# Norm scale applied by a diagonal matrix in the transposes, stores of the normed rows issued by ACT, token rows of the folds loaded beside the second projection

## The chip, the cores and the metric

The kernel runs on one core of a Trainium2 chip. A core has five engines that each work through their own instructions in order: TensorE (PE: matrix products, PEld its weight loads), VectorE (DVE), ScalarE (ACT), GpSimd (POOL) and SyncE (SP, which here only issues transfers). ACT and POOL issue transfers too. The metric is the device time of one execution in microseconds.

## The reference

Two layers of a trunk work on 1280 tokens (1024 of a sample, 256 of a prompt) of width 1024. Layer 0 mixes by differential attention and an RWKV-7 recurrence, layer 1 by a Fourier transform over positions and channels; each layer ends with a gated FFN of inner width 2816. What the change touches are the norms and the residual sums around these:

```python
def rmsnorm(x, g):
    y = xf * lax.rsqrt(jnp.mean(xf * xf, axis=-1, keepdims=True) + RMS_EPS)
    return y * g

def trunk_layer(l, x, mod, rope, ctx, P):
    h = rmsnorm(x, gains[0]) * (1 + scale_m) + shift_m
    if l % 2 == 0:
        m, new_ctx = even_mixer(h, l, rope, ctx, P)
    else:
        m, new_ctx = fourier_mix(h, P["w_out_odd"][l // 2]), None
    x = x + gate_m * rmsnorm(m, gains[1])
    h = rmsnorm(x, gains[2]) * (1 + scale_f) + shift_f
    f = conv_ffn(h, P["w_ffn_in"][l], P["ffn_conv"][l], P["ffn_conv_b"][l], P["w_ffn_out"][l])
    x = x + gate_f * rmsnorm(f, gains[3])
```

## The kernel before

The tokens are worked on in ten blocks of 128 rows, of 1024 elements each. Matrix products are made of three products of a high and a low part (`mm3`, L145 to L147), and the parts are made by `split` (a cast on ACT, L140, and a difference on DVE, L141). A scheduler sets the order of the instructions on every engine from the program's text and the pools' buffers.

Four places matter.

The *output stage of layer 0* (some 1640 to 1760 us) makes the mixer's output `of` for each block, adds it to the token rows, and norms the sum for the FFN: DVE writes the scaled rows to a tile of their own, `nxs` (L292); `norm_store` transposes them in eight blocks of 128x128 into PSUM (L303, `n_ps`); ACT (L307) and DVE (L311) in turn write `nt` from that with the modulation; and POOL stores `nt` to `h_d` in memory (L315). The FFN loads it from there as `tc` (L1260).

The *second projection of each FFN* (in layer 0 some 2380 to 2618 us) goes through three groups of blocks: two of four blocks and one of two. Each group runs over the 22 slices of the inner width; for each slice it loads a piece of the weight (`e_raw`) and of the activations (`e_m`), splits them into `e_hi` and `e_lo`, and adds to accumulators in the PSUM banks a, b, c and d. At a group's end `finish` copies them out (`fo`), norms and gates them, adds the token rows `rx`, and stores the sum.

The *folds* (from 2618 us) open layer 1. Each of five folds loads two blocks of token rows (`nx`), makes the reciprocal norm, builds `dg`, a diagonal matrix of the norms, on POOL (L1630), multiplies the rows by it (`xt_ps`, L1638), copies that out (`fh`) and multiplies it with the transform's table (`ab_ps`, L1650).

The *output stage of layer 1* (some 2720 to 2860 us) runs `outputs` for five pairs of blocks: the prompt's pair first, then the sample's pairs `lt` 0, 3, 1 and 2, in an order of steps written out by hand. Each pair makes a difference `fmn` and a sum `fpl`, gates both, adds `fmn` to the first block's rows (on POOL, L1894) and the flipped `fpl` to the second block's (L1900), and stores both to `x2` (L1895 and L1903; the trace calls the memory `x_d`). L1903 stores from row `s0` on, and `s0` is 1 for the last pair of a sequence:

```python
            s0 = 1 if lt == ntl - 1 else 0
            nc.sync.dma_start(out=x2[t0s[1] + s0:t0s[1] + 128], in_=x[s0:128])
```

That is so for the prompt's pair and for `lt` 3. Here the norm's scale is written over the token rows themselves (L1879), and `norm_store` transposes them from there.

Of the kernel before, what the change touches and what calls it, by code (L numbers as in the profile page):

```python
# [18 lines left out]
D = 1024  # L19
# [12 lines left out]
RING = 5  # L32
# [67 lines left out]
def hybrid_step(ctx: ExitStack, tc: tile.TileContext, i: dict, o: dict):  # L100
# [183 lines left out]

    def norm_scale(pl, tj, f, xs):

        jk = pl.tile([128, D], F32, tag=tj[0], bufs=tj[1], name="njk")
        ss = pl.tile([128, 1], F32, tag="nss", bufs=4, name="nss")
        nc.scalar.activation(jk, f, AF.Square, accum_out=ss)
        rs = pl.tile([128, 1], F32, tag="nrs", bufs=4, name="nrs")  # L290
        rsqrt(rs, ss, 1.0 / D, RMS_EPS, pl, 1)
        nc.vector.tensor_scalar(out=xs, in0=f, scalar1=rs, op0=ALU.mult, scalar2=None)  # L292

    def norm_store(pl, tt, ps_tile, xs, t0, hd, A, B):

# [3 lines left out]
        for k0 in range(0, KD, 4):  # L299
            ps = ps_tile()  # L300
            t = pl.tile([128, 4, 128], F32, tag=tt[0], bufs=tt[1], name="nt")
            for e in range(4):
                nc.tensor.transpose(ps[:, e, :], xs[:, (k0 + e) * 128:(k0 + e + 1) * 128], ident)  # L303
            for e in range(4):
# [5 lines left out]
                else:  # L310
# [3 lines left out]
                    )  # L314
            nc.gpsimd.dma_start(out=hd[half, :, k0:k0 + 4, c:c + n], in_=t[:, :, :n])  # L315

# [337 lines left out]

    def out_product(fw, fo, po, t0, nf=2):

# [623 lines left out]
    with ExitStack() as st:  # L1280
# [6 lines left out]
        for n, j in enumerate((0, 4, 1, 8, 9, 5, 2, 6, 3, 7)):  # L1287
            t0 = j * 128
            f = fs.pop(0) if fs else out_product(fw, fo, po, t0)
            if todo:  # L1290
                norm_store(xp, ("nt", 3), n_ps, *todo.pop(), hd, A, B)
            if n == 6:
                strassen_tokens(opa, xp, hd, 0, 256)
            finish_tile(xp, f, gg, None, lambda a, n: x_d[0][a:a + n], t0)
            xs = xp.tile([128, D], F32, tag="nxs", bufs=2, name="nxs")
            norm_scale(xp, ("njk", 1), f, xs)
            todo.append((xs, t0))

# [8 lines left out]
    def ffn(l, src, dst_rows, st, fw, hd, opa, late, groups, then):  # L1307
# [3 lines left out]
        with st:  # L1311
# [120 lines left out]
            def out_operands(f, js, early):  # L1432

                hl = lambda: [
                    (fw if early else dp).tile(
                        [128, 512], F32R, tag=("f_" if early else "e_") + q, bufs=RING if early else 15, name="e_" + q
                    ) for q in ("hi", "lo")
# [35 lines left out]
            def finish(j, pss):  # L1473
                t0 = j * 128
                f = dp.tile([128, D], F32, tag="fo", bufs=3, name="fo")
                for hf in range(2):
                    nc.scalar.copy(f[:, hf * 512:hf * 512 + 512], pss[hf])
                x = dp.tile([128, D], F32, tag="rx", bufs=4, name="rx")
                nc.sync.dma_start(out=x, in_=x_rows(src, t0, 128))
# [11 lines left out]
            for gi, js in enumerate(groups):  # L1491
                acc = {j: [bank("abcd"[2 * (e % 2) + hf]) for hf in range(2)] for e, j in enumerate(js)}
                tail = gi == len(groups) - 1
                kept = {}
                for f in range(NFF):
                    if gi == 0 and f == 2:
                        st_u.close()
                        st_h.close()
                        beside = then()
                        dp = pool(st, "fd")  # L1500
                        for cnd in range(2):
                            g = dp.tile([128, D], F32, name=f"gg{cnd}")
                            nc.gpsimd.dma_start(out=g, in_=mod_d[l][1, cnd].partition_broadcast(128))
                            gg.append(g)
                    if gi == 0 and f == 6:
                        beside()
                    ops = out_operands(f, js, gi == 0 and f < 2)
                    if tail and f >= NFF - 4:
                        kept[f] = ops
# [58 lines left out]
    def fourier_tables():  # L1568

        ab = pool(st_t, "qa")  # L1570
        bs = pool(st_b, "qb")
        F["A"] = mod_cols(1, 1)
        F["B"] = mod_cols(1, 0)
# [21 lines left out]
    with ExitStack() as st:  # L1595
# [18 lines left out]
        s1 = pool(st_b, "qx")  # L1614
        flip = flip_tile(s1)

        def fold(cnd, n):
# [3 lines left out]
            for m, a in enumerate((base + 1 + 128 * n, base + L - 128 * (n + 1))):  # L1621
                x = s1.tile([128, D], F32, tag="nx", bufs=4, name="nx")
                nc.sync.dma_start(out=x, in_=x1[a:a + 128])
                jk = s1.tile([128, D], BF16, tag="njk", bufs=1, name="njk")
                ss = s1.tile([128, 1], F32, tag="nss", bufs=4, name="nss")
                nc.scalar.activation(jk, x, AF.Square, accum_out=ss)
                rs = s1.tile([128, 1], F32, tag="nrs", bufs=4, name="nrs")
                rsqrt(rs, ss, 1.0 / D, RMS_EPS, s1, 1)
                d = s1.tile([128, 128], F32, tag="dg", bufs=4, name="dg")
                nc.gpsimd.tensor_scalar(out=d, in0=(ident, flip)[m], scalar1=rs, scalar2=None, op0=ALU.mult)  # L1630
# [229 lines left out]
        def outputs(cnd, lt, g, xp, flip):  # L1860
# [3 lines left out]
            t0s = base + l0, base + L - 128 * (lt + 1)  # L1864
            xs = []
            fm = xp.tile([128, D], F32, tag="fmn", bufs=1, name="fmn")
# [10 lines left out]
            def scale(m):  # L1877
                x = xs[m]
                nc.vector.tensor_scalar(out=x, in0=x, scalar1=rms(xp, x), scalar2=None, op0=ALU.mult)  # L1879

            def norm(m):
                norm_store(xp, ("nt", 3), E["n"], xs[m], t0s[m], hd, A, B)

# [9 lines left out]
            gated(xp, fm, g)  # L1893
            nc.gpsimd.tensor_tensor(out=xs[0], in0=xs[0], in1=fm, op=ALU.add)  # L1894
            nc.sync.dma_start(out=x2[t0s[0]:t0s[0] + 128], in_=xs[0])  # L1895
# [114 lines left out]
```

## Time and profile before

| what | value |
| --- | --- |
| runs, us | 3745.22, 3733.98, 3738.79 (median 3738.79) |
| the profiled execution, us | 3751.75 |
| its span, from the first to the last instruction, us | 3749.9 |
| mean granted clock of TensorE | 0.935 of full speed |
| PE busy | 91% of the span |
| DVE busy | 62% |
| ACT busy | 43% |
| POOL busy | 16% |

The profiled execution is one of its own; its time stands beside the span to show what lies around it. Shares of busy time are averages over the whole span. The granted clock is 1.00 at 2.4 GHz and half of that at 1.2 GHz.

### The profile page before, as it was taken

What the parts mean: (1) busy time and instruction counts of PE and PEld (TensorE: products, weight loads), DVE (VectorE), ACT (ScalarE), POOL (GpSimd) and SP (SyncE); (2) the same over time, 40 slices, a digit from 0 to 9 for tenths busy, and PEclk for the clock granted to TensorE, in tenths of its full rate; (3) what the DMA queues carried; (4) which work ended last, traced back from release to release, by engine and by line L of the source; (5) the groups of instructions that cost most, each with busy time, mean ns of one, the idle gap of its engine ahead of it and who ended that gap; (6) DMA issues with size and microseconds to landing.
All of it is one profiled execution on the core that took longest, in us unless ns stands there. A gap on an engine that the chain in (4) does not pass through costs nothing. (4 is left out here: it accounts for less than half of the span.)

```text
span 3749.9 us, 58125 instructions
## 1 busy us (share of the span) xinstructions
PE 3430.5 (91%) x21672; PEld 2914.6 (78%) x21672; DVE 2320.2 (62%) x5039; ACT 1611.7 (43%) x3248; POOL 581.6 (16%) x883
## 2 busy tenths in 40 slices
PE   6999999889898967788999999999875999999999
PEld 5888887655554656667899999887754899999887
DVE  4277677745464657547877776545547877776345
ACT  4266566753444443435433322335434433333334
POOL 3111112421221212022000002201122000001000
PEclk9999999879797967889999999999887999999999
DMA  6322313233243200155222224855335212225455
GB/s 214 99 86 88 94 61 101 69 93 110 90 121 94 79 19 17 55 155 171 90 70 74 65 74 149 263 189 181 131 104 154 89 63 72 73 66 180 143 187 184
DMA packets 313435, 413.83 MB, mean 110 GB/s; under 512 B 62770, under 2 KB 228626, under 8 KB 313152
## 3 DMA queue, kind: packets, MB, share of 16 engines
q1 hardware_dynamic: 234784, 308.58, 26.7%
q0 software_dynamic: 29968, 81.88, 6.3%
q10 hardware_dynamic: 48400, 19.65, 2.1%
q8 instruction: 171, 2.80, 0.3%
q14 instruction: 112, 0.92, 0.1%
HBM read 321.21 MB, written 90.83 MB: 110 GB/s over the span
## 5 line engine op out<-in xcount | busy, mean ns | idle before, releaser
L140 ACT CAST f_hi<-ws 128x512 fp32r<-128x512 f32 x192 | 119.1, 621 | 360.8 <-PE ua_ps L146 156.5
L1392 POOL DMA_DIRECT2D m_d<-md x176 | 95.5, 543 | 1001.3 <-DVE md L1391 1001.1
L141 DVE TENSOR_TENSOR e_lo<-e_m,e_hi 128x512 fp32r<-128x512 f32 (+1 forms) x132 | 79.3, 600 | 247.6 <-ACT e_hi L140 247.6
L140 ACT CAST f_hi<-f_raw 128x512 fp32r<-128x512 f32 x144 | 89.2, 621 | 300.7 <-PE ud_ps L146 106.1
L192 PE MATMUL ada_ps<-ada_w,csil 128*32 128x512 f32 x384 | 174.2, 728 | 27.4 <-DMA ada_w<-in_w_ada 25.9
L145 PE MATMUL f_ps<-hh,w_hi 128*128 128x512 f32 (+1 forms) x552 | 198.5, 360 | 0.5 <-ACT nk L451 0.5
L140 ACT CAST e_hi<-e_m 128x512 fp32r<-128x512 f32 (+1 forms) x132 | 72.6, 550 | 292.0 <-PE uc_ps L147 265.2
L147 PE MATMUL f_ps<-hh,w_lo 128*128 128x512 f32 (+1 forms) x552 | 197.3, 357 | 0.0
L146 PE MATMUL f_ps<-hl,w_hi 128*128 128x512 f32 (+1 forms) x552 | 197.3, 357 | 0.0
L141 DVE TENSOR_TENSOR e_lo<-e_raw,e_hi 128x512 fp32r<-128x512 f32 x264 | 174.0, 697 | 23.3 <-ACT e_hi L140 23.1
L140 ACT CAST e_hi<-e_raw 128x512 fp32r<-128x512 f32 x264 | 151.1, 618 | 61.3 <-DMA e_raw<-in_w_ffn_out 32.5
L141 DVE TENSOR_TENSOR f_lo<-ws,f_hi 128x512 fp32r<-128x512 f32 x192 | 133.7, 697 | 44.6 <-ACT f_hi L140 44.5
L141 DVE TENSOR_TENSOR f_lo<-f_raw,f_hi 128x512 fp32r<-128x512 f32 x144 | 98.9, 688 | 99.8 <-ACT f_hi L140 99.6
L531 DVE TENSOR_REDUCE nm<-sc_ps 128x1 f32<-128x512 f32 (+1 forms) x208 | 118.8, 583 | 54.2 <-PE sc_ps L527 53.1
L532 ACT ACTIVATE e<-sc_ps,nm 128x512 f32<-128x512 f32 (+1 forms) x208 | 126.1, 608 | 56.8 <-DVE nm L531 53.9
L1380 DVE SCALAR_TENSOR_TENSOR cv<-gp,cw,cv 128x1282 f32<-128x1282 f32 x88 | 134.4, 1548 | 0.0
L145 PE MATMUL ua_ps<-b11h,f_hi 128*128 128x256 f32 (+1 forms) x352 | 111.7, 317 | 10.9 <-ACT nt L307 6.4
L145 PE MATMUL ub_ps<-b21h,f_hi 128*128 128x256 f32 (+1 forms) x352 | 111.5, 317 | 8.2 <-ACT b21h L140 7.7
L527 PE MATMUL sc_ps<-ks,qs 128*128 128x512 f32 (+1 forms) x384 | 110.9, 382 | 6.7 <-ACT e L532 6.7
L145 PEld LDWEIGHTS f_ps<-hh,w_hi 128*128 128x128 f32 x552 | 104.2, 189 | 16.2 <-DVE qr L441 1.0
L146 PE MATMUL ua_ps<-b11l,f_hi 128*128 128x256 f32 (+1 forms) x352 | 111.2, 316 | 5.6 <-DVE b11l L141 5.6
L146 PEld LDWEIGHTS f_ps<-hl,w_hi 128*128 128x128 f32 x552 | 104.2, 189 | 14.7 <-issue 0.5
(656 smaller groups left out, 11253.6 us busy)
## 6 DMA issues: line engine op xcount, KB each, us to landing
e_raw<-in_w_ffn_out SPq DMA_DIRECT2D x132, 512.0 KB, 4.2
f_raw<-in_w_ffn_in SPq DMA_DIRECT2D x96, 512.0 KB, 4.0
ada_w<-in_w_ada SPq DMA_DIRECT2D x160, 256.0 KB, 2.9
m_d<-md POOLq DMA_DIRECT2D x88, 192.0 KB, 2.4
w_raw<-in_w_in_even SPq DMA_DIRECT2D x23, 512.0 KB, 5.2
m_d<-md POOLq DMA_DIRECT2D x88, 128.0 KB, 2.0
e_m<-m_d SPq DMA_DIRECT2D x44, 256.0 KB, 4.3
lo_in<-fb_d SPq DMA_DIRECT2D x40, 256.0 KB, 3.0
```

The source lines that it names most:

```text
L140: nc.scalar.copy(hi, src)
L141: nc.vector.tensor_tensor(out=lo, in0=src, in1=hi, op=ALU.subtract)
L145: nc.tensor.matmul(ps, lhsT=a[0], rhs=b[0], start=first, stop=False)
L146: nc.tensor.matmul(ps, lhsT=a[0], rhs=b[1], start=False, stop=False)
L147: nc.tensor.matmul(ps, lhsT=a[1], rhs=b[0], start=False, stop=last)
L192: nc.tensor.matmul(ps[32 * q:32 * q + 32], lhsT=csil[:, k0 + k, :], rhs=w[:, k, :], start=(k0 < 4), stop=(k0 >= 4),)
L527: nc.tensor.matmul(ps[:, :nn], lhsT=qs[:, m, a, :], rhs=ks[m][:, n0:n0 + nn], start=(a == 0), stop=(a == 1),)
L531: nc.vector.reduce_max(nm[:, m, j:j + 1], ps[:, :nn], axis=AX.X, negate=True)
L532: nc.scalar.activation(e[:, :nn], ps[:, :nn], AF.Exp, bias=nm[:, m, j:j + 1], accum_out=sm[:, m, j:j + 1])
L1380: nc.vector.scalar_tensor_tensor(out=cv, in0=gp[:, j:T + 2 + j], scalar=cw[:, j, f + e:f + e + 1], in1=cv, op0=ALU.mult, op1=ALU.add,)
L1392: nc.gpsimd.dma_start(out=m_d[f + e, :, half, c * 256:c * 256 + n], in_=md)
```

## The change

The scale of the norm is no longer written to the rows. `scale_matrix` (layer 0) and `scale` (layer 1) write a 128x128 matrix `dg` with the norms on its diagonal, on DVE, and `norm_store` multiplies the unscaled rows by it, with `matmul` in place of `transpose`. Its stores are issued by ACT instead of POOL. In `outputs` the sum of rows and `fmn` moves from POOL to DVE. In the second projection the ring of operands has 12 buffers instead of 15 (a set is three), `rx` 2 instead of 4, the last group holds back three slices instead of four, a group of two blocks uses the banks c and d alone, and the gates are loaded at slice 4. The folds' token rows and norms get a pool of their own, `qn`, that is opened with the transform's tables, ahead of the second projection's end.

```diff
-    def norm_scale(pl, tj, f, xs):
+    def scale_matrix(pl, tj, f):
...
-        nc.vector.tensor_scalar(out=xs, in0=f, scalar1=rs, op0=ALU.mult, scalar2=None)
+        dg = pl.tile([128, 128], F32, tag="dg", bufs=2, name="dg")
+        nc.vector.tensor_scalar(out=dg, in0=ident, scalar1=rs, scalar2=None, op0=ALU.mult)
+        return dg
...
-                nc.tensor.transpose(ps[:, e, :], xs[:, (k0 + e) * 128:(k0 + e + 1) * 128], ident)
+                nc.tensor.matmul(
+                    ps[:, e, :], lhsT=x[:, (k0 + e) * 128:(k0 + e + 1) * 128], rhs=dg, start=True, stop=True
+                )
...
-            nc.gpsimd.dma_start(out=hd[half, :, k0:k0 + 4, c:c + n], in_=t[:, :, :n])
+            nc.scalar.dma_start(out=hd[half, :, k0:k0 + 4, c:c + n], in_=t[:, :, :n])
...
-    def out_product(fw, fo, po, t0, nf=2):
+    def out_product(fw, fo, po, t0, nf=3):
...
-                        [128, 512], F32R, tag=("f_" if early else "e_") + q, bufs=RING if early else 15, name="e_" + q
+                        [128, 512], F32R, tag=("f_" if early else "e_") + q, bufs=RING if early else 12, name="e_" + q
...
-                x = dp.tile([128, D], F32, tag="rx", bufs=4, name="rx")
+                x = dp.tile([128, D], F32, tag="rx", bufs=2, name="rx")
...
-                acc = {j: [bank("abcd"[2 * (e % 2) + hf]) for hf in range(2)] for e, j in enumerate(js)}
+                acc = {j: [bank(("cd" if len(js) == 2 else "abcd")[(2 * e + hf) % min(4, len(js))]) for hf in range(2)] for e, j in enumerate(js)}
...
+                    if gi == 0 and f == 4:
...
-                    if tail and f >= NFF - 4:
+                    if tail and f >= NFF - 3:
...
+        F["sn"] = pool(st_b, "qn")
...
-                x = s1.tile([128, D], F32, tag="nx", bufs=4, name="nx")
+                x = sn.tile([128, D], F32, tag="nx", bufs=4, name="nx")
...
-                d = s1.tile([128, 128], F32, tag="dg", bufs=4, name="dg")
+                d = sn.tile([128, 128], F32, tag="dg", bufs=4, name="dg")
...
-                x = xs[m]
-                nc.vector.tensor_scalar(out=x, in0=x, scalar1=rms(xp, x), scalar2=None, op0=ALU.mult)
+                d = xp.tile([128, 128], F32, tag="dg", bufs=1, name="dg")
+                nc.vector.tensor_scalar(out=d, in0=ident, scalar1=rms(xp, xs[m]), scalar2=None, op0=ALU.mult)
+                dgs.append(d)
...
-            nc.gpsimd.tensor_tensor(out=xs[0], in0=xs[0], in1=fm, op=ALU.add)
+            nc.vector.tensor_tensor(out=xs[0], in0=xs[0], in1=fm, op=ALU.add)
```

The order of SP's issues in the output stage of layer 1, around the second store of 127 rows, was this (`x_d_60` is `x1`, `x_d_61` is `x2`; `nx` are loads of token rows, `tc` what the FFN reads):

```order
L1890 DMA nx<-x_d_60 128x1024
L1895 DMA x_d_61<-nx 128x1024
L1903 DMA x_d_61<-nx 127x1024
L1260 DMA tc<-h_d_70 128x256
L1890 DMA nx<-x_d_60 128x1024 x2
```

With the change it is this:

```order
L1897 DMA nx<-x_d_60 128x1024
L1264 DMA tc<-h_d_70 128x256
L1902 DMA x_d_61<-nx 128x1024
L1910 DMA x_d_61<-nx 127x1024
L1897 DMA nx<-x_d_60 128x1024 x2
```

The load of `tc` has moved ahead of the store of 127 rows; two loads of token rows stand behind the store in both.

ACT's order from the end of layer 0's second projection to the first fold was this (`rjk` and `njk` are the sums of squares of the projection's and of the folds' norms):

```order
L1477 COPY fo<-uc_ps 128x512
L1488 DMA x_d_60<-fo 128x1024
L1477 COPY fo<-ud_ps 128x512
L1482 ACTIVATE rjk,rss<-fo 128x1024
L1488 DMA x_d_60<-fo 128x1024
L1626 ACTIVATE njk,nss<-nx 128x1024 x4
L1678 ACTIVATE zj,zs<-zx 2x1024
L1723 CAST w64s<-w64r 72x1024
L1645 COPY fh<-xt_ps 128x512 x2
```

With the change it is this:

```order
L1479 COPY fo<-uc_ps 128x512
L1479 COPY fo<-ud_ps 128x512
L1484 ACTIVATE rjk,rss<-fo 128x1024
L1490 DMA x_d_60<-fo 128x1024 x2
L1651 COPY fh<-xt_ps 128x512
L1684 ACTIVATE zj,zs<-zx 2x1024
```

The four norms of the folds and the cast of `w64s` no longer stand between the last store and the copy `fh`.

## Rows read from the trace of the kernel before

**Rows 1.** The page's busy times: engine, us, share of the span, instructions.

```profile
PE 3430.5 (91%) x21672; PEld 2914.6 (78%) x21672; DVE 2320.2 (62%) x5039; ACT 1611.7 (43%) x3248; POOL 581.6 (16%) x883
```

**Rows 2.** Busy time in stretches: length, PE, PEld, DVE, ACT, POOL, clock, DMA share, GB/s.

```profile
1700.00:1720.00 20.00, 20.00 (x96) 16.61 (x95) 14.88 (x35) 11.47 (x29) 4.43 (x7) 1.00 0.69 230
...
2580.00:2600.00 20.00, 20.00 (x90) 16.55 (x89) 13.60 (x26) 11.93 (x25) 0.00 (x0) 1.00 0.93 290
...
2800.00:2820.00 20.00, 6.73 (x23) 5.04 (x24) 5.66 (x11) 5.59 (x13) 5.29 (x6) 0.59 0.25 83
```

**Rows 3.** Waits from 2725 to 2860 us: who for what, total us, times, longest.

```profile
PE n_ps L303 <- ACT nt L307: 41.0, 4, 17.1
PE n_ps L303 <- DVE nx L1879: 10.9, 1, 10.9
...
DVE nx L1879 <- DMA x_d<-nx: 35.5, 4, 19.0
...
ACT b11h L140 <- DMA tc<-h_d: 23.5, 2, 20.7
```

**Rows 4.** Timeline of SP's issues: start us, length us, line, what, count.

```profile
2737.93 0.24 SPq L1903 DMA_DIRECT2D x_d<-nx  x1
...
2787.69 0.24 SPq L1903 DMA_DIRECT2D x_d<-nx  x1
2789.75 7.69 SPq L1260 DMA_DIRECT2D tc<-h_d  x1
2797.54 18.05 SPq L1890 DMA_DIRECT2D nx<-x_d  x2
```

**Rows 5.** Timeline of DVE; in brackets the idle time before and its releaser.

```profile
2761.68 0.75 DVE L1879 TENSOR_SCALAR nx<-nx,nrs 128x1024 f32<-128x1024 f32 x1 [15.31 <-DMA x_d<-nx]
...
2811.08 0.75 DVE L1879 TENSOR_SCALAR nx<-nx,nrs 128x1024 f32<-128x1024 f32 x1 [19.01 <-DMA x_d<-nx]
...
2815.89 1.29 DVE L1853 SCALAR_TENSOR_TENSOR fmn<-fmn,nrs,gg 128x1024 f32<-128x1024 f32 x1 [0.75 <-POOL nrs L137]
```

**Rows 6.** Transfers from 2735 to 2765 us, GB/s in 40 equal slices.

```profile
GB/s 0 344 355 0 5 22 22 33 16 22 22 27 27 27 27 27 22 88 231 287 131 45 28 26 23 26 27 27 27 27 22 27 27 27 27 5 0 0 0 0
```

**Rows 7.** Timeline of PE, at the folds' start and at a run of transposes.

```profile
2631.02 2.07 PE L1638 MATMUL xt_ps<-dg,nx 128*128 128x128 f32 x8 [12.48 <-POOL dg L1630]
...
2639.60 0.79 PE L1650 MATMUL ab_ps<-fcs,fh 128*128 128x128 f32 x2 [2.25 <-ACT fh L1645]
...
2743.53 1.03 PE L303 MATMUL n_ps<-ident,nx 128*128 128x128 f32 x8
```

**Rows 8.** Timeline of ACT and its queue, at the folds' start and later.

```profile
2627.22 0.33 ACTq L1488 DMA_DIRECT2D x_d<-fo  x1
...
2638.97 0.57 ACT L1645 COPY fh<-xt_ps 128x512 f32<-128x512 f32 x1
...
2826.50 5.69 ACTq L1322 DMA_DIRECT2D cw<-in_ffn_conv  x1
```

**Rows 9.** Instructions by line: ns least/median/most, first and last start, form.

```profile
L303 PE MATMUL n_ps<-ident,nxs x72: 270/272/476, 1655.1 to 1741.9; 128*128 128x128 f32 x72
...
L1201 DVE TENSOR_TENSOR of<-of,px x10: 1215/1218/1224, 1646.5 to 1749.7; 128x1024 f32<-128x1024 f32 x10
...
L1638 PE MATMUL xt_ps<-dg,nx x160: 274/275/579, 2631.0 to 2674.7; 128*128 128x128 f32 x160
...
L1879 DVE TENSOR_SCALAR nx<-nx,nrs x10: 732/753/755, 2737.9 to 2881.0; 128x1024 f32<-128x1024 f32 x10
...
L1894 POOL TENSOR_TENSOR nx<-nx,fmn x5: 2360/2392/2657, 2732.6 to 2841.8; 128x1024 f32<-128x1024 f32 x5
```

**Rows 10.** Transposes from 1668 to 1745 us, by line.

```profile
L303 PE MATMUL n_ps<-ident,nxs x56: 270/272/329, 1676.0 to 1741.9; 128*128 128x128 f32 x56
```

**Rows 11.** Stores of `h_d` (L315), from issue to landing.

```profile
DMA to landing us min/median/max: 2.7/3.7/7.1
```

**Rows 12.** Timeline of POOL, the transform's second table.

```profile
2623.24 2.87 POOL L1535 TENSOR_TENSOR fcn<-fcn,mod 128x1024 f32<-128x1024 f32 x1
```

More of the change, by code (lines that the diff above doesn't have):

```diff
@@ L291, in norm_scale, with norm_store @@
         rsqrt(rs, ss, 1.0 / D, RMS_EPS, pl, 1)
-        nc.vector.tensor_scalar(out=xs, in0=f, scalar1=rs, op0=ALU.mult, scalar2=None)
-    def norm_store(pl, tt, ps_tile, xs, t0, hd, A, B):
+        dg = pl.tile([128, 128], F32, tag="dg", bufs=2, name="dg")
+        nc.vector.tensor_scalar(out=dg, in0=ident, scalar1=rs, scalar2=None, op0=ALU.mult)
+        return dg
+    def norm_store(pl, tt, ps_tile, x, dg, t0, hd, A, B):
         cnd, p = (0, t0) if t0 < LS else (1, t0 - LS)
@@ L1294, in hybrid_step @@
             finish_tile(xp, f, gg, None, lambda a, n: x_d[0][a:a + n], t0)
-            xs = xp.tile([128, D], F32, tag="nxs", bufs=2, name="nxs")
-            norm_scale(xp, ("njk", 1), f, xs)
-            todo.append((xs, t0))
+            todo.append((f, scale_matrix(xp, ("njk", 1), f), t0))
     def norm_last(bank):
@@ L1571, in fourier_tables @@
         bs = pool(st_b, "qb")
+        F["sn"] = pool(st_b, "qn")
+        F["sn"].tile([128, 1], F32, tag="nss", bufs=4, name="nss")
         F["A"] = mod_cols(1, 1)
@@ L1614, in hybrid_step @@
         s1 = pool(st_b, "qx")
-        flip = flip_tile(s1)
+        sn = F["sn"]
+        flip = flip_tile(sn)
         def fold(cnd, n):
@@ L1621, in fold @@
             for m, a in enumerate((base + 1 + 128 * n, base + L - 128 * (n + 1))):
-                x = s1.tile([128, D], F32, tag="nx", bufs=4, name="nx")
+                x = sn.tile([128, D], F32, tag="nx", bufs=4, name="nx")
                 nc.sync.dma_start(out=x, in_=x1[a:a + 128])
-                jk = s1.tile([128, D], BF16, tag="njk", bufs=1, name="njk")
-                ss = s1.tile([128, 1], F32, tag="nss", bufs=4, name="nss")
+                jk = sn.tile([128, D], BF16, tag="njk", bufs=1, name="njk")
+                ss = sn.tile([128, 1], F32, tag="nss", bufs=4, name="nss")
                 nc.scalar.activation(jk, x, AF.Square, accum_out=ss)
-                rs = s1.tile([128, 1], F32, tag="nrs", bufs=4, name="nrs")
-                rsqrt(rs, ss, 1.0 / D, RMS_EPS, s1, 1)
-                d = s1.tile([128, 128], F32, tag="dg", bufs=4, name="dg")
+                rs = sn.tile([128, 1], F32, tag="nrs", bufs=4, name="nrs")
+                rsqrt(rs, ss, 1.0 / D, RMS_EPS, sn, 1)
+                d = sn.tile([128, 128], F32, tag="dg", bufs=4, name="dg")
                 nc.gpsimd.tensor_scalar(out=d, in0=(ident, flip)[m], scalar1=rs, scalar2=None, op0=ALU.mult)
@@ L1864, in outputs @@
             t0s = base + l0, base + L - 128 * (lt + 1)
-            xs = []
+            xs, dgs = [], []
             fm = xp.tile([128, D], F32, tag="fmn", bufs=1, name="fmn")
@@ L1877, in scale @@
             def scale(m):
-                x = xs[m]
-                nc.vector.tensor_scalar(out=x, in0=x, scalar1=rms(xp, x), scalar2=None, op0=ALU.mult)
+                d = xp.tile([128, 128], F32, tag="dg", bufs=1, name="dg")
+                nc.vector.tensor_scalar(out=d, in0=ident, scalar1=rms(xp, xs[m]), scalar2=None, op0=ALU.mult)
+                dgs.append(d)
             def norm(m):
-                norm_store(xp, ("nt", 3), E["n"], xs[m], t0s[m], hd, A, B)
+                norm_store(xp, ("nt", 3), E["n"], xs[m], dgs[m], t0s[m], hd, A, B)
             half(0)
```

## The prediction

> **What bounds the kernel now.** I read the busy times first, then the busy time by stretches of 20 us, then the waits inside the stretches that fall short, then the single waits in order of time. TensorE is busy for 3430.5 of 3749.9 us [rows 1], so what counts is where it stops. In the second projection of the first layer's FFN it is busy for 20.00 of 20 us at full clock, with the DMA engines at 0.93; in the first layer's output stage it is also at 20.00 of 20 [rows 2]. Nothing in those two places may get later. The loose place is the second layer's output stage (2720 to 2860 us): the stretch from 2800 has 6.73 us of TensorE at a granted clock of 0.59 [rows 2].
>
> The waits of that stage say why [rows 3]. TensorE stands 41.0 us, 4 times, at `n_ps` for ACT's `nt`, and 10.9 us for DVE's `nx`; DVE stands 35.5 us for the store `x_d<-nx`; ACT stands once for 20.7 us for `tc<-h_d`. They are one story, told in the order of time by the timeline. DVE scales the token rows in place, so it must wait until the store of the same rows has read them. Most of these stores are short, but two move 127 rows instead of 128. The first is issued at 2737.93 and DVE goes on at 2761.68 after 15.31 us; the second is issued at 2787.69 and DVE goes on at 2811.08 after 19.01 us [rows 4, 5]. From issue to release that is 23.75 and 23.39 us. While the first runs the DMA engines move only 22 to 33 GB/s for most of the time [rows 6]. What SP issues behind the second one sticks too: the load of `tc` at 2789.75 has an issue of 7.69 us, and two loads of token rows fill 18.05 us from 2797.54 [rows 4].
>
> A second loose place is the start of the folds: TensorE's first `xt_ps` matmul waits 12.48 us for `dg` from 2618.54 to 2631.02, and its first `ab_ps` matmul starts at 2639.60, after ACT's copy `fh` at 2638.97 [rows 7, 8].
>
> **The change, part by part.**
>
> *Second layer's output stage.* The scale becomes `dg = ident * rs`, which writes no token row, so neither 15.31 nor 19.01 us has a reason left on DVE. TensorE bounds the gain. It had other work during the first wait and stood 10.9 us of it [rows 3]; of its four waits for `nt` the longest, 17.1 us [rows 3], lies beside the second (by its length: the other three share 23.9). Upper end: 10.9 + 17.1 = 28 us. What is late next is the second store itself. It has the same 127 rows, the loads of the next pair of row blocks (`lt` 1) stand right behind it on SP, and the order puts `tc` ahead of it now. If everything up to it comes 10.9 us earlier, it is issued at 2776.8 and, with 23.4 us, ends at 2800.2. DVE's sum `nx + fmn` then waits for rows that stuck behind it. That end is 10.9 us earlier than 2811.08; and the two gates that ran after the wait, the last ending at 2815.89 + 1.29 = 2817.18 [rows 5], can run ahead of it. Of these 6.1 us I count 5.6, since the rows land a little after the store. Lower end: 5 us, if the wait for rows holds DVE as long as the old wait did. I take 10.9 + 5.6 = **16.5 us less**.
>
> *POOL's sum moves to DVE.* 2392 ns on POOL become about 1218 ns on DVE, by the same sum elsewhere [rows 9], 5 times; and ten scales of 753 ns become ten `dg`. A 128x128 scale on DVE from SBUF is not in the rows; it lies between nothing and the 753 ns of the scale with eight times the columns [rows 9]; I take 0.3 us, since a part of the cost will not shrink with the columns. Where DVE stands in the chain that is up to 5 x 1.17 + 10 x 0.45 = 10 us; most lies beside TensorE's work or under the waits that I have counted. I take **2 us less** (0 to 4 beyond the waits).
>
> *Transposes become matmuls.* The same kind of matmul stands in the folds: 160 records of 275 ns for 80 instructions, so each runs twice over the array, against one record of 272 ns for one transpose [rows 9]. Eight transposes in a run take 1.03 us at full clock [rows 7], so they are (1.03 - 0.27) / 7 = 0.109 us apart. One more pass is 0.109 us; 160 of them are 17.4 us of TensorE if all were on its path. In the output stage of layer 0 seven tiles of 8 (56 records) lie between 1676 and 1742 us [rows 10], where TensorE is at 20.00 of 20 [rows 2]: 7 x 0.87 = **6.1 us more**. The other 13 tiles stand where TensorE waits for eviction anyway, which hides them; without that cover they are 11.3 us more.
>
> The Trainium skill (Perfetto Trace Analysis, Transposes) says that a logical transpose should be a transpose instruction and not a standard matmul. The two passes in the row agree that the matmul costs more; charged everywhere, the rule would make the sum 11.3 us worse.
>
> *Stores of `h_d` on ACT.* 40 issues leave POOL. They land in 2.7 to 7.1 us [rows 11]. On ACT a store stands right behind the `nt` that it stores, which saves POOL's turn, but ACT's queue holds the table loads `cw`, one of which occupies the issuing queue for 5.69 us [rows 8]; stores behind it wait, and what loads `tc` for the FFN waits for them. The issue that leaves POOL saves nothing by itself, since POOL is not on the path; I count 0, with 3 us either way in each layer, less than one landing.
>
> The Trainium skill (DMA: Bandwidth & Descriptors, Issuing engines are not separate DMA queues) says that another issuing engine saves only the sequencer's time, since all end on the same 16 DMA engines. No run here shows it yet for these stores; by it the term is 0 as well.
>
> *Second projection.* Rings go from five operand sets to four, `rx` from 4 to 2 buffers, the two-token group uses two banks' pairs only, the folds' four loads come beside it. 90 matmuls in 20 us [rows 2] are 0.222 us each; one step of the two-token group has 12, 2.7 us, so four sets are 10.8 us ahead, five 13.5. The step needs 640 KB; DMA is at 0.93 and 290 GB/s in the last group [rows 2], and 2 MB of token rows at that rate are 7.2 us of DMA time. At each group's change the first tokens need banks that are copied late. I take **2 us more** for both layers together: nothing below (TensorE cannot be faster than 20.00 of 20), 7.2 above.
>
> *Folds.* Rows, norms and four `dg` are done before the last matmul, so the first `xt_ps` can follow at 2618.5. Then ACT's `fh` copy holds it: in the new order it stands behind both stores of `fo`, and the second of these came at 2627.22 [rows 8]. So `fh` starts at 2627.22 + 0.33 = 2627.55 instead of 2638.97: **11.4 us less**. POOL's table product ends at 2623.24 + 2.87 = 2626.11 [rows 12], before that. Bounds: 0, if the loads come too late, to 13 (12.48 and a little clock). The later folds keep their pace.
>
> Sum: -16.5 - 2 + 6.1 + 0 + 2 - 11.4 = **-21.8 us** on the profiled execution's 3751.75 us (the span and 1.85 us around it), to 3730. That execution was 12.96 us above the median of the runs; -0.58% of 3738.79 is **3717 us**. About 0.3% (11 us) is what a measurement of this kernel can tell from no change.
>
> **Rivals.**
>
> *The wait comes back under another name.* The 127-row store lasts as before; rows for the next pair and ACT's cast of `tc` wait behind it, and the output stage gains only 5. Sum -10.3, 3728 us. For it: SP's queue is in order, and the loads filled 18.05 us behind the store [rows 4]. Against: DVE's other work goes first. The Trainium skill (DMA: Bandwidth & Descriptors, Why a DMA increments its semaphore by 16 and not by 1) says that 127 partitions put a transfer on one DMA engine; the 22 to 33 GB/s agree, and by it the store stays as long as it is.
>
> *Everything opens.* Output stage -28, folds -13, sums -4, the extra passes hidden by later evictions: -45, 3694 us. Against: the full stretch at 1700 has no slack.
>
> *Slower: the second projection runs out of operands.* One mechanism: four sets and the nearly full DMA engines hold the steps of the two-token groups back. There are 22 steps in each layer, 44 in all. The gains elsewhere are 21.8 + 2 = 23.8; it decides from 23.8 / 44 = 0.54 us on each 2.7 us step. At 0.8 us it is 35.2 - 23.8 = +11.4, 3750 us. For it: DMA at 0.93 [rows 2]. Against: 640 KB at 290 GB/s are 2.2 us of the 2.7, and the extra rows are one burst of 7.2 us.
>
> *The folds' part doesn't do what it says* (their loads still wait): -10.4, again 3728.
>
> **How the numbers follow.** My forecast (within 10 us of -21.8) gets 0.45, the returned wait 0.20, everything open 0.17, the folds not moved 0.08, slower 0.10. Faster by over 0.3%: 0.42 of the first, 0.17, and a third of the two at -10: 0.69. Slower by over 0.3%: the last, 0.10. The rest, 0.21, is within 0.3%. The range goes from 3692 (just under everything open) to 3742 (the operands short by 0.6 us a step).
>
> **What would show it.** In the new profile DVE's 35.5 us for `x_d<-nx` must be gone; if my step is right, DVE or ACT wait instead for `nx<-x_d` behind the second 127-row store, and TensorE's waits at `n_ps` fall from 52 to some 30 us. The first `xt_ps` starts within 3 us of the last matmul and the first `ab_ps` near 11 us earlier than before, relative to that matmul. Records of the transposes double. TensorE stays at 20.00 of 20 in the second projection. The prediction is wrong if TensorE shows waits there, if `nt` waits for stores on ACT's queue, or if the layer-0 output stage grows by more than 10 us.

## The result and the profile after

| | median, us | lowest to highest | runs |
| --- | --- | --- | --- |
| before, on the same chip | 3737.38 | 3728.24 to 3745.22 | 7 |
| changed | 3715.44 | 3706.24 to 3727.19 | 7 |

The ratio is 0.9946, with a 95% interval of 0.9927 to 0.9966: 20 us less (13 to 27). The changed kernel's profiled execution took 3722.7 us, 29.05 us less than that of before; some 7 us of those are that the earlier one lay further above its median (14.4 us against 7.3).

First the page's span and busy times (answer to [rows 1]), then the stretches that answer to [rows 2], with those of layer 1's output stage from 2720 us on. Columns as there.

```profile
span 3720.9 us, 58403 instructions
...
PE 3441.2 (92%) x21832; PEld 2932.1 (79%) x21832; DVE 2317.2 (62%) x5044; ACT 1609.4 (43%) x3248; POOL 532.2 (14%) x838
```

```profile
1700.00:1720.00 20.00, 18.51 (x88) 14.63 (x87) 15.88 (x42) 13.63 (x34) 3.49 (x4) 1.00 0.73 226
...
2560.00:2580.00 20.00, 17.99 (x80) 14.58 (x79) 15.72 (x24) 9.73 (x20) 2.74 (x3) 1.00 0.95 323
2580.00:2600.00 20.00, 20.00 (x90) 16.56 (x89) 13.12 (x25) 12.85 (x26) 1.16 (x2) 1.00 0.90 297
...
2720.00:2740.00 20.00, 20.00 (x93) 15.16 (x91) 13.04 (x23) 9.35 (x19) 3.15 (x6) 1.00 0.35 129
2740.00:2760.00 20.00, 20.00 (x105) 16.10 (x105) 12.70 (x29) 10.57 (x22) 3.30 (x6) 1.00 0.41 120
2760.00:2780.00 20.00, 20.00 (x100) 16.18 (x99) 10.16 (x20) 8.14 (x16) 2.20 (x4) 1.00 0.43 132
2780.00:2800.00 20.00, 6.91 (x35) 4.99 (x33) 7.53 (x16) 4.95 (x10) 1.31 (x8) 0.75 0.33 115
```

TensorE has 160 records more and 11 us more of busy time, in a shorter span. The first wait in the output stage has gone (2720 to 2780 is full); one long hole is left, from 2780. The second projection has got a small dent at 2560. What the waits say in that output stage, in the order TensorE (from 2690 us on), DVE and ACT (2700 to 2860 us; answer to [rows 3]):

```profile
PE n_ps L305 <- ACT nt L311: 23.6, 3, 13.6
...
DVE nx L1901 <- DMA nx<-x_d: 11.2, 1, 11.2
DVE nt L315 <- DMA h_d<-nt: 10.4, 3, 3.6
...
ACT b11h L140 <- DMA tc<-h_d: 2.8, 2, 1.7
```

DVE's 35.5 us for `x_d<-nx` are gone, and TensorE's 51.9 us at `n_ps` are 23.6. In their place DVE stands 11.2 us for token rows, `nx<-x_d`. SP's timeline and DVE's show where (answer to [rows 4, 5]), and the transfers from 2765 to 2805 us, in slices of 1 us, what went on meanwhile (answer to [rows 6]):

```profile
2762.96 0.33 SPq L1264 DMA_DIRECT2D tc<-h_d  x1
...
2767.36 0.24 SPq L1910 DMA_DIRECT2D x_d<-nx  x1
2767.72 10.54 SPq L1897 DMA_DIRECT2D nx<-x_d  x2
```

```profile
2793.75 1.22 DVE L1901 TENSOR_TENSOR nx<-nx,fmn 128x1024 f32<-128x1024 f32 x1 [11.17 <-DMA nx<-x_d]
```

```profile
GB/s 373 16 0 12 16 52 221 220 85 23 28 23 146 314 227 343 80 155 130 242 65 26 27 28 23 28 23 28 24 25 91 406 29 225 299 303 277 263 316 368
```

The second store of 127 rows starts at 2767.36, the rows for the next pair stand behind it, and DVE has them at 2793.75, 26 us later. For nine slices the engines move 23 to 28 GB/s, as before. `tc` went ahead of the store; ACT waits 2.8 us for it in place of 23.5.

The folds' start (PE and ACT; answer to [rows 7, 8]), and the prices of the new instructions (answer to [rows 9, 11]):

```profile
2620.20 1.95 PE L1644 MATMUL xt_ps<-dg,nx 128*128 128x128 f32 x16
2629.80 0.80 PE L1656 MATMUL ab_ps<-fcs,fh 128*128 128x128 f32 x2 [7.65 <-ACT fh L1651]
```

```profile
2628.79 0.33 ACTq L1490 DMA_DIRECT2D x_d<-fo  x1
2629.16 0.59 ACT L1651 COPY fh<-xt_ps 128x512 f32<-128x512 f32 x1 [6.99 <-DVE z L1697]
```

```profile
L305 PE MATMUL n_ps<-dg,of x144: 270/275/377, 1655.7 to 1741.4; 128*128 128x128 f32 x144
...
L1885 DVE TENSOR_SCALAR dg<-ident,nrs x10: 276/278/287, 2728.0 to 2862.7; 128x128 f32<-128x128 f32 x10
...
L319 ACTq DMA_DIRECT2D h_d<-nt x40: 366/367/5151, 1663.4 to 2869.0; - x40
...
DMA to landing us min/median/max: 2.3/3.2/15.2
```

144 records stand where there were 72. A `dg` takes 0.278 us. A store of `h_d` costs ACT 0.367 us to issue, but one took 5.151, at 2801.78 between the table loads `cw`. One landed after 15.2 us: it is one of the two issued from 2736.67 on, behind the first store of 127 rows (2729.00) and long before the tables.

**The time by stages.** Whole executions spread by some 20 us; stages between two fixed matmuls tell more. The marks are the first start of the first `o_ps` product, of the first FFN product `ua_ps<-b11h`, of the first product of the second projection `ua_ps<-e_hi`, of the first `pq_ps<-fclsh,ab0ch` (which reads the folds' results), and the last start of `ua_ps<-b11h`, which ends the second layer's first projection. For the kernel before, and then for the changed one (columns as in [rows 9]):

```profile
L145 PE MATMUL o_ps<-o_hi,oyhi x160: 388/389/796, 1601.3 to 1738.6; 128*128 128x512 f32 x160
...
L145 PE MATMUL ua_ps<-b11h,f_hi x352: 277/336/689, 1748.6 to 3419.6; 128*128 128x256 f32 x88, 128*128 128x384 f32 x88
L145 PE MATMUL ua_ps<-e_hi x220: 389/389/397, 2319.1 to 3733.7; 128*128 128x512 f32 x110
...
L145 PE MATMUL pq_ps<-fclsh,ab0ch x8: 278/283/387, 2682.1 to 2718.9; 128*128 128x258 f32 x4, 128*128 128x256 f32 x4
```

```profile
L145 PE MATMUL o_ps<-o_hi,oyhi x160: 387/389/796, 1603.0 to 1739.0; 128*128 128x512 f32 x160
...
L145 PE MATMUL ua_ps<-b11h,f_hi x352: 277/336/690, 1748.1 to 3390.3; 128*128 128x256 f32 x88, 128*128 128x384 f32 x88
L145 PE MATMUL ua_ps<-e_hi x176: 389/389/397, 2318.7 to 3648.6; 128*128 128x512 f32 x176
...
L145 PE MATMUL pq_ps<-fclsh,ab0ch x8: 278/283/386, 2672.0 to 2710.4; 128*128 128x258 f32 x4, 128*128 128x256 f32 x4
```

The same marks in every run below, one profiled execution each, in us; the last column is the ratio of the times to the kernel before on the same chip, with its interval:

| kernel | layer 0 output stage | first projection | second projection and folds | layer 1 output stage to the end of its first projection | rest | ratio |
| --- | --- | --- | --- | --- | --- | --- |
| before | 147.3 | 570.5 | 363.0 | 737.5 | 330.3 | 1 |
| changed | 145.1 | 570.6 | 353.3 | 718.3 | 330.6 | 0.9946 (0.9927 to 0.9966) |
| changed again (`c0_after`) | 143.8 | 570.3 | 354.1 | 718.1 | 330.7 | 0.9950 (0.9934 to 0.9965) |
| `e1_inplace` | 144.0 | 570.0 | 353.7 | 734.5 | 330.9 | 0.9989 (0.9972 to 1.0006) |
| `e2_split_before` | 142.9 | 568.1 | 362.0 | 702.8 | 330.2 | 0.9913 (0.9889 to 0.9936) |
| `e3_split_after` | 144.4 | 571.2 | 354.6 | 703.4 | 330.5 | 0.9895 (0.9875 to 0.9915) |
| `e5_folds_late` | 145.1 | 570.4 | 359.2 | 718.4 | 331.0 | 0.9960 (0.9946 to 0.9974) |
| `e4_pool_stores` | 141.7 | 571.7 | 353.4 | 717.0 | 330.6 | 0.9918 (0.9893 to 0.9944) |
| `e6_layer0_scaled` | 137.8 | 569.2 | 354.3 | 718.0 | 330.7 | 0.9911 (0.9891 to 0.9931) |
| `e11_cw_rows` | 142.9 | 570.3 | 352.8 | 711.6 | 330.9 | 0.9914 (0.9893 to 0.9936) |
| `e10_split_cw_rows` | 140.5 | 570.0 | 354.3 | 695.8 | 330.7 | 0.9863 (0.9842 to 0.9885) |
| `e13_nf2` | 149.6 | 570.9 | 356.9 | 719.0 | 330.6 | 0.9955 (0.9938 to 0.9972) |
| `e14_all` | 136.9 | 568.0 | 352.5 | 696.7 | 330.4 | 0.9852 (0.9827 to 0.9877) |
| `e15_all_pool` | 134.2 | 570.5 | 352.1 | 700.6 | 329.9 | 0.9875 (0.9852 to 0.9897) |

How far a stage of the same code spreads can be read off the table: the layer 0 output stage is 143.8 to 145.1 in the five kernels that have the changed kernel's code there, and 147.3 and 142.9 in the two that have the code of before; second projection and folds are 352.8 to 354.6 in eight that have the changed kernel's code there, 356.9 in a ninth (`e13_nf2`), and 363.0 and 362.0 with the code of before; the layer 1 stage is 718.0 to 719.0 in five. The profile of before lies 14.4 us above its median and that of the changed kernel 7.3, so these two rows differ in sum by some 7 us more than the medians do. Ratios stand against runs of the kernel before on the same chip; for `e4_pool_stores`, `e6_layer0_scaled`, `e11_cw_rows` and `e10_split_cw_rows` that median was 3746.82 us, against 3737.38 to 3739.95 us for the others, so between these groups the stages are the better measure.

### The profile page after: what moved, and what is told of

Same layout as the page of the kernel before. It is cut to its first block, busy times and chain, and to the rows that moved or that the text cites. A ratio compares the mean times of both kernels' runs of the same rounds, so it can differ in the third digit from the quotient of the medians.

```text
span 3720.9 us, 58403 instructions
## 1 busy us (share of the span) xinstructions
PE 3441.2 (92%) x21832; PEld 2932.1 (79%) x21832; DVE 2317.2 (62%) x5044; ACT 1609.4 (43%) x3248; POOL 532.2 (14%) x838
## 5 line engine op out<-in xcount | busy, mean ns | idle before, releaser
L145 PE MATMUL ua_ps<-b11h,f_hi 128*128 128x256 f32 (+1 forms) x352 | 111.8, 318 | 14.4 <-ACT b11h L140 8.0
L145 PE MATMUL ub_ps<-b21h,f_hi 128*128 128x256 f32 (+1 forms) x352 | 111.2, 316 | 10.9 <-ACT b21h L140 10.3
L145 PEld LDWEIGHTS f_ps<-hh,w_hi 128*128 128x128 f32 x552 | 104.2, 189 | 16.2 <-DVE qr L445 1.0
## 6 DMA issues: line engine op xcount, KB each, us to landing
m_d<-md POOLq DMA_DIRECT2D x88, 128.0 KB, 2.0
```

The lines of the kernel that those rows point to most:

```text
L145: nc.tensor.matmul(ps, lhsT=a[0], rhs=b[0], start=first, stop=False)
```

## The experiments

**Back to the scale in place, in layer 1 alone (`e1_inplace`).**

```diff
-                d = xp.tile([128, 128], F32, tag="dg", bufs=1, name="dg")
-                nc.vector.tensor_scalar(out=d, in0=ident, scalar1=rms(xp, xs[m]), scalar2=None, op0=ALU.mult)
-                dgs.append(d)
+                x = xs[m]
+                nc.vector.tensor_scalar(out=x, in0=x, scalar1=rms(xp, x), scalar2=None, op0=ALU.mult)
+                dgs.append(None)
```

(`None` makes `norm_store` use the transpose instruction, so the second passes of layer 1 go as well.)

> The changed kernel, but layer 1's scale is written over the token rows again and its blocks are transposed by the transpose instruction. Theory (DVE waits for the store of 127 rows only because it overwrites what the store reads): DVE stands 30 us or more for x_d<-nx again, the output stage of layer 1 loses some 18 us against the changed kernel, and what is left against the kernel before is the folds' part, about 10 us (ratio near 0.997). Rival (the gain of that stage comes from the new order, from DVE's sum or from the stores on ACT): the wait stays short, and the ratio stays near the changed kernel's 0.9946.

DVE's waits in the output stage of this kernel:

```profile
DVE nx L1888 <- DMA x_d<-nx: 34.0, 3, 19.9
```

The wait is back with 34.0 us, the stage is 734.5 us, 16.2 more than in the changed kernel, and the ratio is 0.9989. DVE's sum, the new order and the stores on ACT are all still in this kernel; together they are worth 3 us of the stage. The rival falls. The ratio leaves 4 us of gain, with an interval of -2 to 10, where some 10 were expected; the stage with the folds is 9.3 us shorter than in the profile of before.

**Only the store's shape, in the kernel before (`e2_split_before`).**

```diff
-            nc.sync.dma_start(out=x2[t0s[1] + s0:t0s[1] + 128], in_=x[s0:128])
+            for r0, r1 in ((1, 113), (113, 128)) if s0 else ((0, 128),):
+                nc.sync.dma_start(out=x2[t0s[1] + r0:t0s[1] + r1], in_=x[r0:r1])
```

> The kernel before, in which each store of 127 rows is issued as one of 112 rows and one of 15. Theory (the store's 23.4 us are those of its shape, and the in-place scale is harmless beside a quick store): each part lands in some 2.5 to 5 us, DVE's 35.5 us for x_d<-nx fall under 8, and the kernel gains 18 to 28 us by itself (ratio 0.9925 to 0.995), as much as the changed kernel does as a whole, without any of its parts. Rival (a slow stretch of all transfers there, whatever the shape): the stores stay above 15 us and the ratio is 1.000.

DVE's wait in that stage, and the transfers from 2714 to 2734 us in slices of 0.5 us (the first store of this shape is issued at 2717.10):

```profile
DVE nx L1879 <- DMA x_d<-nx: 1.1, 2, 0.7
```

```profile
GB/s 0 0 377 401 270 0 0 90 279 287 344 90 0 0 0 0 0 16 0 0 0 0 0 0 0 0 73 293 164 293 219 0 0 0 0 0 0 0 0 0
```

The 508 KB go through in some 2.5 us at up to 344 GB/s, where one transfer of 127 rows needed over 23 us. The in-place scale is still there and waits 1.1 us. The stage is 34.7 us shorter than in the kernel before, nearly twice the changed kernel's gain, and the ratio of 0.9913, 29 us less by the medians, is better than expected. The rival falls: it was the shape. The 112 rows start at row 1 as the 127 did, so it was the number of rows and not the row that they start at.

**The same in the changed kernel (`e3_split_after`)**, with the diff of the run before.

> The changed kernel with the same split of the stores of 127 rows. Theory (the next wait in its output stage is DVE's 11.2 us for nx<-x_d, whose loads stand behind the second store on SP): that wait goes, the stage gains a further 8 to 13 us, ratio 0.991 to 0.993 against the kernel before. Rival (the queue behind ACT's table loads and h_d stores bounds the stage's end anyway): the wait goes, but the first FFN products start at the same time, and the ratio stays within 0.001 of 0.9946.

TensorE's waits at `n_ps` in that stage are down from 23.6 us:

```profile
PE n_ps L305 <- ACT nt L311: 10.9, 2, 8.7
```

No wait for `nx<-x_d` is left, and DVE's 10.4 us for stores of `h_d` on ACT's queue are 0.5:

```profile
DVE nt L315 <- DMA h_d<-nt: 0.5, 1, 0.5
```

The longest time from issue to landing of such a store falls from 15.2 to 4.1 us, with the table loads still on that queue. The stage is 14.9 us shorter than in the changed kernel, somewhat more than expected, and it is 703.4 us where the kernel before with the same split has 702.8. So with a quick store the diagonal matrix, the sum on DVE and the stores on ACT together give layer 1's output stage nothing. What the change then still gives is the folds' part (354.6 against 362.0 us); the medians, 3701.24 against 3710.03 us, differ by 9, though the intervals of the two ratios overlap.

**The folds' rows late again (`e5_folds_late`).**

```diff
-        F["sn"] = pool(st_b, "qn")
-        F["sn"].tile([128, 1], F32, tag="nss", bufs=4, name="nss")
...
-        sn = F["sn"]
+        sn = s1
```

> The changed kernel with the folds' token rows in the later pool again, so that their loads wait for the second projection's end. Theory: the first ab_ps matmul starts some 20 us after the last matmul of the projection instead of 9.6, the kernel loses 9 to 11 us against the changed kernel (ratio 0.997 to 0.998 against before), and DMA in the last group's stretch falls. Rival (the folds' gap is hidden by what follows, or the early loads cost in the projection what they give): ratio within 0.001 of 0.9946.

The timeline of PE at the folds' start:

```profile
2630.67 3.44 PE L1642 MATMUL xt_ps<-dg,nx 128*128 128x128 f32 x16 [12.29 <-POOL dg L1634]
2634.49 0.49 PE L1654 MATMUL ab_ps<-fcs,fh 128*128 128x128 f32 x2 [0.38 <-ACT fh L1649]
```

The wait for `dg` is back with 12.29 us, but the first `ab_ps` matmul follows 16.1 us after the last matmul of the projection (2618.38 by this wait), not 20. The stage is 5.9 us longer than in the changed kernel, about 60% of what I had expected. By this pair of profiles the early loads are thus worth some 6 us of the 9.7 (4.6 to 6.4 against eight of the nine), and the rest comes with the other edits around the second projection, which this run doesn't part. The time itself (0.9960 against 0.9946) doesn't tell the two kernels apart.

**The stores of `h_d` on POOL (`e4_pool_stores`).**

```diff
-            nc.scalar.dma_start(out=hd[half, :, k0:k0 + 4, c:c + n], in_=t[:, :, :n])
+            nc.gpsimd.dma_start(out=hd[half, :, k0:k0 + 4, c:c + n], in_=t[:, :, :n])
```

> The changed kernel with the stores of h_d issued by POOL again. Theory (in the changed kernel ACT's queue hurts: DVE stands 10.4 us for h_d<-nt, and a store's issue takes 5.15 us between the table loads cw): that wait shrinks, but the waits for nx<-x_d and for cw stay and most of the 10.4 us lies beside them, so the time changes by less than 4 us either way (ratio 0.9935 to 0.9955 against before). Rival 1 (the stores on ACT are a gain of their own): 5 us or more slower than the changed kernel. Rival 2 (they cost): 5 us or more faster.

Layer 0's output stage is 141.7 us (2.1 and 3.4 us less than in the two profiles with the stores on ACT) and layer 1's 717.0 (1.3 less). Its ratio, 0.9918, lies below the range expected, but its interval overlaps that of the changed kernel, and the median of before that it stands against is some 7 us above the others. Neither rival: who issues these stores is worth no more than 5 us, with a lean to POOL.

**One pass for each transpose in layer 0 (`e6_layer0_scaled`).**

```diff
-            todo.append((f, scale_matrix(xp, ("njk", 1), f), t0))
+            xs = xp.tile([128, D], F32, tag="nxs", bufs=2, name="nxs")
+            norm_scale(xp, ("njk", 1), f, xs)
+            todo.append((xs, None, t0))
```

> The changed kernel, but in layer 0 the scaled rows go to a tile of their own again and are transposed by the transpose instruction, with one pass for each block of 128x128 instead of two. Theory (the second passes did cost TensorE 0.87 us a tile in layer 0's output stage, and other waits that fell hid it): from the first o_ps matmul to the first FFN matmul it is 3 to 6 us shorter than the changed kernel's 145.1 us, ratio about 0.993. Rival (passes are free there, since TensorE waits for loads and evictions over the stage as a whole): 145 us within 1.5, or longer, ratio 0.9946.

The stage is 137.8 us, 6.0 to 7.3 us less than in the two profiles of the changed kernel. The second passes do cost TensorE what the rows of before gave, 6.1 us, and more than DVE's shorter scale gives back: within the stage TensorE is busy for 125.9 us, against 133.7 and 132.2 in the two profiles of the changed kernel and 128.0 in the kernel before. The rival falls.

**Two buffers for `of` (`e13_nf2`).**

```diff
-    def out_product(fw, fo, po, t0, nf=3):
+    def out_product(fw, fo, po, t0, nf=2):
```

> The changed kernel with two buffers instead of three for the output tile of of layer 0's output stage. Theory (the 6 to 7 us of second passes were given back because the third buffer lets TensorE and ACT run ahead, so that the wait for prs and for of fell): the stage from the first o_ps matmul to the FFN grows from 145 to 149 us or more. Rival (the new order of DVE's work, with a short dg in place of the scale, gave it back): the stage stays within 2 us of 145.

TensorE's waits from 1595 to 1765 us:

```profile
PE o_ps L145 <- ACT of L674: 3.5, 1, 3.5
PE n_ps L305 <- DVE dg L293: 3.1, 1, 3.1
```

In the changed kernel on the same chip (`c0_after`) they are 2.3 us for `of` and 1.0 for `dg`. The stage is 149.6 us, 5.8 more than there: TensorE stands idle in it for 15.1 us instead of 11.6, and is busy for 134.5 instead of 132.2. With two buffers the code of before is idle for 19.3 us (15.4 in `e2_split_before`). So the third buffer gave back about what the second passes took, with one profile of this run to show it; the ratios, 0.9955 and 0.9950, do not part the two kernels.

**The tables `cw` in rows (`e11_cw_rows`).**

```diff
-            for j in range(3):
-                nc.scalar.dma_start(out=cw[:, j, :], in_=i["ffn_conv"][l, j].rearrange("(k p) -> p k", p=128))
-            nc.scalar.dma_start(out=cw[:, 3, :], in_=i["ffn_conv_b"][l].rearrange("(k p) -> p k", p=128))
+            craw = wu.tile([128, 512], F32, tag="ws", bufs=2, name="cw_raw")
+            nc.scalar.dma_start(out=craw[0:3 * NFF, 0:128], in_=i["ffn_conv"][l].rearrange("j (k p) -> (j k) p", p=128))
+            nc.scalar.dma_start(out=craw[3 * NFF:4 * NFF, 0:128], in_=i["ffn_conv_b"][l].rearrange("(k p) -> k p", p=128))
+            cps = bank("a")
+            nc.tensor.transpose(cps[:, 0:4 * NFF], craw[0:4 * NFF, 0:128], ident[0:4 * NFF, 0:4 * NFF])
+            nc.scalar.copy(cw.rearrange("p j k -> p (j k)"), cps[:, 0:4 * NFF])
```

> The changed kernel, with the convolution's tables cw loaded as 88 rows of 512 bytes in two transfers per layer and turned by one transpose and one copy, instead of four transfers of single elements on ACT's queue. Theory (cw on ACT's ring holds the h_d stores and ACT itself at the FFN's start): ACT's stretch of store and table issues from 2801 to 2816 us shrinks to a few us, TensorE's longest wait for nt, 13.6 us, falls under 6, and the kernel gains 6 to 12 us against the changed kernel (ratio 0.9915 to 0.993). Rival (the FFN's start waits for loads of tc and weights whatever ACT does): ratio within 0.001 of 0.9946.

ACT's queue around one `h_d` store, first in the changed kernel, then in this one:

```profile
2800.95 0.73 ACTq L1324 DMA_DIRECT2D cw<-in_ffn_conv  x1
...
2801.78 5.15 ACTq L319 DMA_DIRECT2D h_d<-nt  x1
```

```profile
2790.54 1.35 ACTq L1324 DMA_DIRECT2D cw_raw<-in_ffn_conv  x1
...
2791.99 0.37 ACTq L319 DMA_DIRECT2D h_d<-nt  x1
```

The store behind the table load no longer takes 5.15 us to issue but 0.37. The stage is 6.7 us shorter. The theory was half right: TensorE's longest wait for `nt` stays (13.7 us). That one belongs to the store of 127 rows: with both mended, in the next run, the longest is 4.8 us.

**Both (`e10_split_cw_rows`).**

> The changed kernel with both: the split of the stores of 127 rows and cw in rows. Theory (two separate waits, one behind the other): the gains add, 12 to 20 us under the changed kernel, ratio 0.9855 to 0.988 against before. Rival (after the split the stage's end is bound by the same chain that cw's removal would shorten, or by tc): no more than the split alone, ratio 0.9895.

```profile
PE n_ps L305 <- ACT nt L311: 4.8, 1, 4.8
```

The stage is 695.8 us: 22.5 less than in the changed kernel, and 14.9 + 6.7 = 21.6 was the sum of the two. They add.

**The changed kernel as a measure (`c0_after`).**

> The changed kernel itself, as the measure for the three others on the same chip. Expected: ratio 0.9946 within its interval (0.993 to 0.9965); its stages as in its first profile (145 us from the first o_ps matmul to the FFN, 353 us from the second projection to the first pq_ps, 718 us from there to the end of the second layer's first projection), each within 3 us.

0.9950 (0.9934 to 0.9965), all stages within 1.3 us of the first profile.

**All of them (`e14_all`)**: the diffs of `e3_split_after`, `e11_cw_rows` and `e6_layer0_scaled`, and the two-token group's banks as before:

```diff
-                acc = {j: [bank(("cd" if len(js) == 2 else "abcd")[(2 * e + hf) % min(4, len(js))]) for hf in range(2)] for e, j in enumerate(js)}
+                acc = {j: [bank("abcd"[2 * (e % 2) + hf]) for hf in range(2)] for e, j in enumerate(js)}
```

> The changed kernel with the stores of 127 rows split, the tables cw in rows, layer 0's blocks scaled into a tile of their own and transposed by the transpose instruction, and the two-token group on the banks a to d again. Theory (each of these is a wait or a pass of its own): 22 us for the second layer, 7 us for layer 0's output stage, 2 us at the change to the last group (TensorE's wait uc_ps<-fo gone; the stage from the second projection to pq_ps 351 to 352 us), sum -31 us against the changed kernel, ratio 0.985 to 0.988 against before. Rival (they take from one another): ratio 0.9863 as with the first two alone, or the last group's end runs later because the folds find their banks taken.

The median is 3681.92 us, ratio 0.9852 (0.9827 to 0.9877): faster than both kernels. Against `c0_after` the stages give -6.9, -2.3, -1.6 and -21.4 us, -32 in all. The second projection has no wait `uc_ps<-fo` any more; the folds start no later.

**The same with the stores on POOL (`e15_all_pool`).**

> The same with the stores of h_d issued by POOL. Theory (the issuing engine doesn't matter once cw is off ACT's queue): within 4 us of the one before in every stage. Rival (stores on POOL free ACT and help by 3 us in each output stage, as the run with POOL's stores alone seemed to show): 4 to 8 us less.

2.7 us less in layer 0's output stage, 3.9 more in layer 1's; 0.9875 (0.9852 to 0.9897). No gain: the theory holds.

## Why the prediction was right

3717 us were forecast and 3715.44 measured. By its steps:

*Layer 1's output stage: right.* -16.5 and -2 were forecast, -19.2 measured (-19.4 in the second profile). `e1_inplace` shows the cause: 16.2 us come back with the scale in place alone. The replacement came where it was put: rows behind the second store of 127 rows, 11.2 us on DVE. The store was to start 10.9 us earlier, at 2776.8; in the new profile it starts at 2767.36, which is 2777.5 on the old scale, since the folds had ended 10.1 us earlier. Of TensorE's 51.9 us at `n_ps` some 30 were to be left, and 23.6 were. Priced at nothing, and named as a sign of being wrong, were waits of `nt` for stores on ACT's queue: DVE has 10.4 us of them. `e4_pool_stores`, where that wait is 0.5 us and the stage only 1.3 us shorter, shows that they lie beside other waits; in `e3_split_after` it is 0.5 us too, so what held these stores was again the store of 127 rows.

*Folds and second projection: right in sum.* -11.4 and +2 were forecast, -9.7 measured. The first `ab_ps` came 9.6 us after the last matmul against 21.1 before, 11.5 less, and was held, as forecast, by ACT's `fh` behind the second store of `fo`. That store waits for DVE's gate and sum of the last block, which take 2.91 and 2.80 us (1.28 and 1.22 for the block before it) while POOL makes `fcs` and `fcn`; no run tests whether POOL is the reason. The +2 is the wait `uc_ps<-fo` in layer 0's projection, 2.0 us in the dent at 2560; it goes with the banks in `e14_all`. A wait of TensorE there was named as a sign of being wrong; it came, no larger than its price. The mis-sized part is inside: the early loads alone are some 6 us, not 11.4.

*Layer 0's output stage: the term was right, the stage was not.* +6.1 was forecast for the second passes; the pair of profiles has -2.2, and over all profiles (142.9 and 147.3 against 143.8 to 145.1) the stage is the same within its spread. The passes cost 6 to 7 us, as `e6_layer0_scaled` shows. What I left out is the third buffer of `of`, an edit of one number that I gave no price; `e13_nf2` puts it at 5.8 us. I had read the stage as full from the stretch at 1700 alone; TensorE had waits ahead of it and behind it, which a buffer could take away. In the kernel before:

```profile
1660.00:1680.00 20.00, 15.89 (x66) 13.02 (x67) 12.10 (x23) 11.75 (x25) 7.74 (x12) 0.76 0.77 240
...
PE n_ps L303 <- DVE prs L135: 5.9, 1, 5.9
...
PE n_ps L303 <- DVE nxs L292: 1.7, 1, 1.7
```

In the changed kernel the same stretch is full and the granted clock there is 1.00 instead of 0.76; in place of these two waits stands a short one for `dg`:

```profile
1660.00:1680.00 20.00, 20.00 (x113) 17.35 (x113) 13.53 (x28) 13.41 (x28) 3.93 (x7) 1.00 0.90 282
...
PE n_ps L305 <- DVE dg L293: 0.3, 1, 0.3
```

*Stores on ACT: right.* Priced at 0 with 3 us either way in each layer; `e4_pool_stores` and `e15_all_pool` differ from their pairs by -3 to +4 us in a stage, with both signs.

The missed 6 to 8 us in layer 0 are not seen in the total: the stages of the pair add to -31 us, the medians differ by 22, and single profiled executions spread by as much. That the total came within 2 us of the forecast is therefore in part luck; with layer 0 as it was measured, the same sum gives some -28 to -30 us.

Of the rivals, the one that the wait comes back under another name was true in kind and smaller in size: it left 11.2 us on DVE where the old wait was 19.0, and the stage gained 19.2 us, not 5. What the prediction says of the 127 rows (the store stays as long as it is) held: DVE had the rows behind it 26 us after its issue. It took the store as given; the runs show that the store was the cause, and that 112 and 15 rows are worth 34.7 us of the stage without the change.

## What to carry to other kernels

When an engine waits long for a transfer, look at the transfer before moving the engine: its GB/s beside its neighbours' and the shape that sets it apart. Here avoiding the wait gave 16 us and left the next reader behind the same store; two issues in place of one gave 35 us of the stage and 29 of the whole time. Price every edit of a diff, also a buffer count, by the wait that it takes away: the cheapest line of this change hid the cost of its main idea in layer 0.

## What the runs showed of the hardware

- A store of 127 rows of 4 KB on SP's queue moves at 22 to 33 GB/s for most of its time and takes over 23 us (23.4 and 23.8 in the kernel before); the same bytes as 112 and 15 rows go through in some 2.5 us (`e2_split_before`). Loads issued behind it on the same queue come late: 18.1 us is the median from issue to landing of the row loads in the window from 2765 to 2805 us of the changed kernel.
- It holds up another queue too. Stores of `h_d` issued on ACT's queue took up to 15.2 us to land in the changed kernel and up to 4.1 with the store split (`e3_split_after`); issued by POOL they took up to 7.1 (the kernel before, `e4_pool_stores`).
- Table loads of single elements on ACT's queue hold the issue of the next store there: 5.15 us instead of 0.37 with the tables in rows (`e11_cw_rows`).
- A 128x128 matmul of 4-byte numbers with a diagonal matrix leaves two records where the transpose instruction leaves one (144 against 72 for layer 0's `n_ps`), and the output stage of layer 0 is 6.0 to 7.3 us longer with it (`e6_layer0_scaled`).
